# ScalarE casts ahead of their step's own work, modulation rows and residual chains at other steps, in a fused transformer layer

## The chip, the core and the metric

The kernel runs on one core of one Trainium2 chip. The metric is the device time of one execution in microseconds (us). A core has engines that run side by side, each through its own instructions in strict order: TensorE (PE in the profile, its weight loads PEld), VectorE (DVE), ScalarE (ACT), GpSimd (POOL) and SyncE (SP), which issues the DMA transfers. They wait for each other by semaphores.

## The reference, cut to what matters

One layer over 1024 latent tokens and 256 context tokens of width 1024, in float32: a half-weighted SwiGLU feed-forward block, attention of two kinds with gates and an output projection, and a second half-weighted SwiGLU block. Each sub-layer is normalised before and after, and shifted, scaled and gated by rows worked out from a conditioning vector ("modulation", nine rows of 1024 for each of the two streams).

```python
def _rmsnorm(x, g):
    y = x * lax.rsqrt(jnp.mean(x * x, axis=-1, keepdims=True) + RMS_EPS)
    return y * g
def _modnorm(x, g_pre, shift, scale):
    return _rmsnorm(x, g_pre) * (1 + scale) + shift
def _residual(x, y, g_post, gate, weight):
    return x + weight * gate * _rmsnorm(y, g_post)
def _swiglu(h, w1, w3, w2):                      # h @ w1, h @ w3: 1024 x 2816, w2: 2816 x 1024
    return (jax.nn.silu(h @ w1) * (h @ w3)) @ w2
```

The first block is applied to latents and to context, then one input projection of both, then the attention, the merge, and the second block on the latents.

## The kernel before, in words

**Products.** Each float32 operand is split into a high part (rounded to the format that TensorE multiplies at full rate, named fp32r in the profile) and a low part, the remainder. A product is three: high by high, high by low, low by high (`mm3`, L159). The split (`split_to`, L200) is two instructions: ScalarE casts the high part, VectorE then subtracts it from the source for the low part, so the second waits for the first. The latent products go by a Strassen-like scheme on 2 by 2 blocks with seven products for eight: a `Unit` (L497) stands for one weight tile pair, has the products `first`, `p6`, `second`, `p5`, `p7`, `p3`, `p4`, the differences t1 to t4 of its weight blocks (`sum`, on VectorE) and the splits of them and of blocks 11, 21 and 22.

**One order, written out by hand.** There is no scheduler: every instruction is pinned to its place in its engine's order. A `Plan` (L164) holds a list of main steps, mostly one product each, and for each step side work (`spread`), and `run` issues a step's main work and behind it the step's side work. Step numbers below are positions in the first plan:

| steps | stage | matmuls of a step |
|---|---|---|
| 0–36 | lead products of the first feed-forward block (ffn1) | 12 of 128x512 |
| 37–154 | ffn1's rest: 22 units, 5 steps each where led, else 7 (`plan_rest`, L636) | 12 of 128x512 |
| 155–231 | ffn1's down quarters: 7 quarters of 11 products over 4 banks (`Quarters`, L757) | 12 of 128x512 |
| 232–275 | context up: 22 column tiles by two matrices (`ctx_up`, L1082) | 24 of 128x256 |
| 276–319 | context down (`ctx_down`) | 6 of 128x512 |
| 320–424 | lead and rest of the input projection, 15 units | 12 of 128x512 |

The second plan later runs ffn2 in the same manner (22 units, then down quarters).

**Side work near the change.** In `plan_rest` a unit's `before` and `within` (L545 ff.) lay the splits and differences behind the steps of the unit before and of itself: both halves of a split stand behind the step's own work. That own work is, after the product, VectorE's sum out of a bank and, by `emit`, a Silu, Sigmoid or copy on ScalarE, which waits for that sum. `Quarters.plan` (L842 ff.) lays the split of operand n three steps ahead of product n, `Quarters.out` adds a finished quarter out of its bank on VectorE. In context up `ctx_split` splits a 128x1024 weight tile three steps ahead. `ada_steps` (L349) is the work on one modulation row: 23 entries, of which 16 load a 128x512 tile of the conditioning matrix and as many multiply-and-add it on VectorE (one instruction for each of the two streams; two entries behind its load), then `add_up` (small products into a bank and a copy out), then `turn`. Row 2 runs in ffn1's rest, row 4 at steps 185 to 231, row 3 at 234 to 268 with bank "v". The residual chains (`residual_steps`, L670; placed by `pos`) put a finished tile of 128 tokens through norm, gate and residual, and norm again: squares on ScalarE, two small instructions on POOL (mean and power), two 128x1024 instructions on VectorE, then the same for the second norm. Chains 0 to 3 stand at steps 210, 213, 216, 219, chains 4 to 7 at 229, 232, 235, 238. Banks carry the names bm, bv, bs, tiles the names of their pools: xv (16 wide), t (half tiles of 512), xu (units).

Of the kernel before, what the change touches and what calls it, by code (L numbers as in the profile page):

```python
# [9 lines left out]
F32R = mybir.dt.float32r  # L10
BF16 = mybir.dt.bfloat16
AF = mybir.ActivationFunctionType
ALU = mybir.AluOpType
# [17 lines left out]
NP = NF // 2  # L31
# [7 lines left out]
def f32(ap):  # L39
    return ap.bitcast(F32)  # L40
# [3 lines left out]
def hybrid_block(ctx: ExitStack, tc: tile.TileContext, a: dict, out: bass.AP):  # L44
# [11 lines left out]
    def nm(s):  # L56
        count[0] += 1
        return f"{s}_{count[0]}"
# [8 lines left out]
    def U(dt=F32, key="u"):  # L67
        return pools[key].tile([P, 1024], dt, tag="u", name=nm("x" + key))
# [7 lines left out]
    def T2(dt=F32, n=512):  # L76
        return pools["t"].tile([P, n], dt, tag="t", name=nm("t"))
# [34 lines left out]
    class Engine:  # L112


        def __init__(self, e):
            self.e = e
# [23 lines left out]
    def flush(before=None):  # L140
        while waiting and (before is None or waiting[0][0] <= before):
            put(*waiting.pop(0)[1:])
# [8 lines left out]
    vec, act, pool = Engine(nc.vector), Engine(nc.scalar), Engine(nc.gpsimd)  # L151
# [12 lines left out]
    class Plan:  # L164


        def __init__(self):
            self.main, self.side = [], {}

        def step(self, *fs):  # L170
            self.main += fs
# [2 lines left out]
        def spread(self, steps, first, last):  # L174

            for x, f in enumerate(steps):
                self.side.setdefault(first + x * (last - first) // len(steps), []).append(f)

        def run(self):
            for i, f in enumerate(self.main):  # L180
                clock[0] = i
                f()
                for g in self.side.pop(i, ()):
                    g()
                while deferred:
                    deferred.pop(0)()
                if owed:
                    owed.pop(0)()
                flush(i)
            assert not self.side  # L190
            clock[0] = None
            flush()

    def duo(n=512, key="u"):
        if key == "t":
            return T2(F32R)[:, :n], T2(F32R)[:, :n]
        t = U(F32R, key)
        return t[:, :n], t[:, 512:512 + n]

    def split_to(hi, lo, src):  # L200
        act.copy(hi, src)
        vec.tensor_tensor(lo, src, f32(hi), op=ALU.subtract)
        return hi, lo

    def split(src, n=512, key="u"):

        return split_to(*duo(n, key), src)

    def split2(src, key="u"):

        return split_to(U(F32R, key), U(F32R, key), src)
# [137 lines left out]
    def ada_steps(ms, tag="v"):  # L349

        s = []
        cur = {}

        def step(m, k, h):
            if m not in cur:
                cur[m] = AdaSum(m, tag)
            if k:
                cur[m].step(k - 1, h)
            if k < KD:
                cur[m].load(k, h)  # L360

        def end(m):
            cur[m].turn()
            if m == 4:
                cols["a1"] = scale_col("a1", 4, 2, 2)
            if m == 7:
                cols["a2"] = scale_col("a2", 7, 4, 1)

        for m in ms:
            s += [lambda m=m, k=k, h=h: step(m, k, h) for k in range(KD + 1) for h in range(2)]  # L370
            s += [lambda: None] * 2 + [lambda m=m: cur[m].add_up(), lambda: None, lambda m=m: end(m)]
        return s
# [124 lines left out]
    class Unit:  # L497
# [5 lines left out]

        def __init__(self, h, srcs, emit):
            self.h, self.srcs, self.emit = h, srcs, emit
            self.w, self.r = {}, {}
            self.led, self.fix = False, None

        def load(self, x, key="u"):
# [8 lines left out]
                self.m1 = T2()  # L518
                ld(self.m1, self.md)

        def split(self, name, key="u"):
            b = {"11": (0, 0), "21": (0, 1), "12": (1, 0), "22": (1, 1)}
            if name in b:
                x, o = b[name]
                src = self.r[x][:, o * 512:(o + 1) * 512]
            else:
                src = self.t[int(name[1]) - 1]
            self.w[name] = split(src, key=key)

        def sum(self, i):  # L530

# [12 lines left out]

        def before(self):  # L545

            first = {} if self.led else {"p7": lambda: self.split("11"), "p4": lambda: self.split("21")}
            return [("p5", lambda: self.sum(1)), ("p7", lambda: self.sum(2)), ("p7", lambda: self.split("t2")),
                    ("p3", lambda: self.split("t1")), ("p3", lambda: self.sum(3)), ("p4", lambda: self.split("t3"))] \
                + list(first.items())  # L550

        def within(self):

            return [("p6", lambda: self.sum(4)), ("p6", lambda: self.split("22")), ("p5", lambda: self.split("t4"))]

        def prod(self, bank, left, right, start, f=None, ks=range(4)):
            hi, lo = self.w[right]
# [78 lines left out]
    def plan_rest(plan, units):  # L636

        for i, u in enumerate(units):
            o = len(plan.main)
            e = plan.step(*u.rest())  # L640
            at = lambda n: o + u.names.index(n)
            for n, f in (u.within() if i else []) + (units[i + 1].before() if i + 1 < len(units) else []):
                plan.spread([f], at(n), at(n) + 1)
            if i + 2 < len(units):
                plan.spread([lambda v=units[i + 2], x=x: v.load(x) for x in (2, 0, 1)], e - 3, e)

# [110 lines left out]
    class Quarters:  # L757
# [12 lines left out]

        def __init__(self, w2, gated, ys):
            self.w2, self.gated, self.ys = w2, gated, ys
            self.b, self.ra, self.sp = {}, {}, {}
            self.n = 7 * NP

        def slot(self, name, p):
# [11 lines left out]
            t = self.ra[n] = T2()  # L788
            ld(t, self.gated.d[self.ORDER[n // NP][0], n % NP])

        def split(self, n, key="v"):
            a = split(self.ra.pop(n), key=key)
            self.sp[n] = a, split(self.slot(self.ORDER[n // NP][1], n % NP), key=key)

        def sum(self, name, p):
            out, x, y = {"t1": ("t1", "b12", "b11"), "t3": ("t3", "b22", "b12"),
# [45 lines left out]
        def plan(self, plan, ahead=3, loads=4):  # L842

            o = len(plan.main)
            at = lambda n: o + n
            for n in range(self.n):
                plan.spread([lambda n=n: self.load_a(n)], at(n) - ahead - loads, at(n) - ahead - loads + 1)
                x = min(at(n) - ahead, at(self.n - self.LAST) - 1)
                plan.spread([lambda n=n: self.split(n)], x, x + 1)
                plan.step(lambda n=n: self.step(n))  # L850
            for p in range(NP):
                for name, first in (("b11", 0), ("b21", NP), ("b12", 9), ("b22", 2 * NP + 2)):
                    x = at(first + p) - ahead - loads
                    plan.spread([lambda name=name, p=p: self.load_b(name, p)], x, x + 1)
                for name, x in (("t1", 4 + 4 * p // 3), ("t2", 2 * NP - 1 + 6 * p // 5), ("t3", 3 * NP + p), ("t4", 4 * NP - 1 + p)):
                    plan.spread([lambda name=name, p=p: self.sum(name, p)], at(x), at(x) + 1)
            return o
# [38 lines left out]
    first = [PB("s") for _ in range(3)]  # L896
# [22 lines left out]
    class Raw:  # L919

        us, f = {}, {}
# [57 lines left out]
    part = {}  # L979
# [37 lines left out]
    plan = Plan()  # L1017
# [24 lines left out]
    o = len(plan.main)  # L1042
# [22 lines left out]
    d1_at = down1.plan(plan)  # L1065
# [8 lines left out]
    cw, cr, cg, cc, cu = {}, {}, {}, {}, {}  # L1074

    def ctx_load(f, x):
        cr[f, x] = load(a[("f1w1", "f1w3")[x]][f], key="v")

    def ctx_split(f, x):
        cw[f, x] = split2(cr.pop((f, x)))  # L1080

    def ctx_up(f, x):  # L1082
        o = PB("m")[:, :NCTX]
# [45 lines left out]
        cols[f"g{v}"] = gate_rows(gcol[v], *x)  # L1129

    o = d1_at + 4 * NP
    plan.spread(ada_steps((4,)), d1_at + 30, d1_at + 7 * NP - 1)
    plan.spread([lambda v=v: gcol.update({v: gate_col(2, 1, v, 0.5)}) for v in range(2)], o + 2, o + 3)
    plan.spread([lambda: gate1(0, "u", "v")], o + 4, o + 5)
    e = len(plan.main)
# [4 lines left out]
    up_at = len(plan.main)  # L1140
    for f, x in ups:
        o = len(plan.main)
        plan.spread([lambda f=f, x=x: ctx_load(f, x)], o - 6, o - 5)
        plan.spread([lambda f=f, x=x: ctx_split(f, x)], o - 3, o - 2)
        plan.step(lambda f=f, x=x: ctx_up(f, x))
    down_at = len(plan.main)
    for e in range(2):
        for f in range(NF):
            o = len(plan.main)
            plan.spread([lambda f=f, e=e: ctx_wload(f, e)], o - 8, o - 7)  # L1150
            plan.spread([lambda f=f, e=e: ctx_wsplit(f, e)], o - 4, o - 3)
            plan.step(lambda f=f, e=e: ctx_down(f, e))
    plan.spread(ada_steps((3,)), up_at + 2, down_at - 8)
    plan.spread([lambda: gate1(1, "v")], down_at + 36, down_at + 37)
    pos = {}
    for j in range(4):
        pos[j] = d1_at + 5 * NP + 3 * j
        pos[4 + j] = up_at - 3 + 3 * j
    pos[8], pos[9] = len(plan.main) + 1, len(plan.main) + 2
    x1s = DR([NLAT, D])  # L1160
    xcs = DR([NCTX, D])
# [93 lines left out]
    for p in range(3):  # L1255
        punits.append(Unit(h2, [cq_src(2 * p), cq_src(2 * p + 1)],
                           lambda i, ci, x, bank, p=p: emit_cq(2 * p + i, ci, x, bank)))

    o = len(plan.main)
# [147 lines left out]
    o = len(plan.main)  # L1407
# [5 lines left out]
    for x, (c, s, ts) in enumerate(sets):  # L1413
        o = len(plan.main)
# [239 lines left out]
    o = va_at  # L1654
# [8 lines left out]
    o = len(plan.main)  # L1663
# [3 lines left out]
    o = len(plan.main)  # L1667
# [3 lines left out]
    o = len(plan.main)  # L1671
# [4 lines left out]
    o = len(plan.main)  # L1676
# [379 lines left out]
    plan = Plan()  # L2056
# [4 lines left out]
    for d in range(KD):  # L2061
        o = len(plan.main)
# [21 lines left out]
    plan = Plan()  # L2084
# [21 lines left out]
    at = {}  # L2106
# [8 lines left out]
    o = len(plan.main)  # L2115
# [13 lines left out]
    o = len(plan.main)  # L2129
# [62 lines left out]
    for j in range(4):  # L2192
        o = d2_at + 5 * NP + 2 * j
        plan.spread([lambda j=j: done2(j, 0)], o, o + 1)
        plan.spread([lambda j=j: done2(j, 1)], o + 1, o + 2)
        o = e - 9 + j
        plan.spread([lambda j=j: done_half(4 + j, 1)], o, o + 1)
        o = e - 4 + j
# [83 lines left out]
```

## Time and profile before

| what | value |
|---|---|
| median of the runs | 2597.57 us (2595.28 to 2597.59, 3 runs) |
| profiled execution | 2596.1 us |
| its span | 2594.3 us |
| mean granted TensorE clock | 0.998 |
| DMA over the span | 464.52 MB, mean 179 GB/s |

The profile is one execution on the chip. Its page gives each engine's busy time, and groups of instructions by line. Nearly every instruction of the other engines is recorded by one helper, L120, and nearly every matmul by L154, so groups are told apart by their tiles ("out<-in", with buffer numbers left out). Square brackets in a timeline give the idle time ahead of an instruction and what ended it. A line "A <- B" of the waits gives total us, times and longest us that engine and line A waited for B. Matmuls are pipelined and their ends are modelled, so a wait reads a little short where a matmul stands ahead of it.

### The profile page before, as it was taken

The page shows a single profiled execution, that of the slowest core. Times are in us where ns is not written, and L with a number is a line of the kernel's source. Part 1 is how long each engine was busy: PE and PEld are TensorE (multiplying, and loading weights), DVE is VectorE, ACT ScalarE, POOL GpSimd, SP SyncE. Part 2 cuts the span into 40 slices and gives each one's busy share as a digit, 9 for nine tenths or more (in the row PEclk, how much of TensorE's full clock was granted, in tenths as well). Part 3 has the DMA queues.
Part 4 walks back from the last instruction along what each step waited for, and adds up shares of the span by engine and source line. Part 5 has one row for each costly group of instructions (what it writes and reads, how often), then busy time and mean ns, then how long its engine had stood idle before and what let it go on. Part 6 is the DMA issues. An engine that isn't in the chain of part 4 may idle for free.

```text
span 2594.3 us, 38254 instructions
## 1 busy us (share of the span) xinstructions
PE 2548.6 (98%) x13464; PEld 2166.9 (84%) x13464; DVE 1885.7 (73%) x3552; ACT 1246.2 (48%) x2362; POOL 224.3 (9%) x368
## 2 busy tenths in 40 slices
PE   8999999999999999999999999999999999999998
PEld 6887778887899888789889999997788888888887
DVE  4788886679686577784469988886535788767777
ACT  6622223446544663333338977773246322323444
POOL 1000000002100000001003522221021000000003
PEclk9999999999999999999999999999999999999999
DMA  8445443935573576665987733206325444336814
GB/s 304 164 172 190 165 157 122 324 110 171 204 281 121 189 253 211 225 195 178 289 306 280 241 94 76 68 13 221 121 98 195 150 159 162 111 107 221 282 59 175
DMA packets 236976, 464.52 MB, mean 179 GB/s; under 512 B 29488, under 2 KB 70640, under 8 KB 236784
## 3 DMA queue, kind: packets, MB, share of 16 engines
q1 hardware_dynamic: 236784, 462.08, 52.6%
q8 instruction: 106, 1.74, 0.3%
q14 instruction: 86, 0.70, 0.1%
HBM read 341.33 MB, written 120.65 MB: 178 GB/s over the span
## 4 chain that ended last, share of the span: by engine, by line
PE 61%; issue 25%; DVE 7%; ACT 5%; DMA 1%; POOL 1%; SPq 0%; DVEq 0%; ACTq 0%; POOLq 0%
PE bs L154 25%; PE bm L154 20%; PE bv L154 12%; PE bm L157 2%; DVE t L120 2%; DVE xu L120 1%; ACT xu L1862 1%; DVE xv L120 1%; DVE xu L1726 1%; DVE t L1889 1%; ACT t L1888 1%; ACT xu L120 1%; PE bs L157 1%; POOL st L120 1%; ACT t L120 1%
## 5 line engine op out<-in xcount | busy, mean ns | idle before, releaser
L154 PE MATMUL bm<-xu,xu 128*128 128x512 f32 (+2 forms) x1584 | 368.8, 387 | 1.0 <-ACT t L120 0.9
L120 ACT CAST xu<-t 128x512 fp32r<-128x512 f32 (+1 forms) x282 | 167.1, 599 | 421.9 <-DVE t L120 405.3
L154 PE MATMUL bs<-xv,xu 128*128 128x512 f32 x1488 | 358.7, 390 | 8.3 <-DVE t L120 8.3
L154 PEld LDWEIGHTS bm<-xu,xu 128*128 128x128 f32 x1584 | 290.2, 188 | 59.1 <-ACT t L120 2.2
L154 PEld LDWEIGHTS bs<-xv,xu 128*128 128x128 f32 x1488 | 278.0, 188 | 71.5 <-issue 9.2
L154 PE MATMUL bv<-xv,xu 128*128 128x512 f32 x1342 | 335.7, 389 | 0.2
L154 PEld LDWEIGHTS bv<-xv,xu 128*128 128x128 f32 x1342 | 251.6, 188 | 53.2 <-issue 1.0
L120 DVE TENSOR_TENSOR xu<-t,xu 128x512 fp32r<-128x512 f32 (+1 forms) x282 | 187.9, 667 | 137.9 <-ACT xu L120 137.9
L154 PE MATMUL bs<-xv,xv 128*128 128x512 f32 x1014 | 250.6, 393 | 4.6 <-DVE xv L120 4.6
L154 PE MATMUL bs<-xu,xu 128*128 128x512 f32 (+1 forms) x1008 | 234.2, 382 | 0.6 <-DVE t L120 0.6
L120 DVE TENSOR_TENSOR xu<-xu,xu 128x512 fp32r<-128x512 f32 (+1 forms) x272 | 185.5, 688 | 60.3 <-ACT xu L120 59.9
L154 PEld LDWEIGHTS bs<-xv,xv 128*128 128x128 f32 x1014 | 190.6, 189 | 44.6 <-issue 5.4
L154 PEld LDWEIGHTS bs<-xu,xu 128*128 128x128 f32 x1008 | 184.1, 188 | 38.2 <-issue 2.2
L120 DVE TENSOR_TENSOR t<-t,t 128x512 f32<-128x512 f32 (+2 forms) x262 | 174.5, 673 | 50.1 <-ACT t L120 46.0
L154 PE MATMUL bs<-w,w 96*128 96x512 f32 (+3 forms) x832 | 206.3, 366 | 2.4 <-DVE st L1751 1.9
L120 POOL TENSOR_SCALAR st<-st 128x1 f32<-128x1 f32 (+1 forms) x66 | 38.6, 584 | 1922.0 <-ACT t L120 1906.9
L120 ACT ACTIVATE t<-t 128x512 f32<-128x512 f32 (+1 forms) x94 | 57.3, 610 | 232.0 <-DVE t L120 228.1
L120 ACT CAST xv<-t 128x512 fp32r<-128x512 f32 x154 | 95.7, 621 | 151.9 <-PE bv L154 65.5
L154 PE MATMUL bm<-t,xu 128*128 128x256 f32 (+1 forms) x1272 | 162.4, 289 | 4.3 <-DVE xu L120 2.7
L154 PE MATMUL bm<-xv,xv 128*128 128x512 f32 x618 | 165.1, 391 | 0.0
L154 PEld LDWEIGHTS bm<-t,xu 128*128 128x128 f32 x1272 | 158.2, 193 | 7.8 <-DVE xu L120 3.5
L154 PE MATMUL bv<-t,w 128*128 128x256 f32 x896 | 151.5, 288 | 2.5 <-DVE t L1889 1.8
(235 smaller groups left out, 4238.2 us busy)
## 6 DMA issues: line engine op xcount, KB each, us to landing
d<-t SPq DMA_DIRECT2D x338, 256.0 KB, 2.4
t<-d SPq DMA_DIRECT2D x246, 256.0 KB, 3.3
xu<-in_f1w SPq DMA_DIRECT2D x59, 512.0 KB, 3.9
xu<-in_f2w SPq DMA_DIRECT2D x58, 512.0 KB, 3.6
t<-in_wada SPq DMA_DIRECT2D x112, 256.0 KB, 3.9
xv<-in_f1w SPq DMA_DIRECT2D x44, 512.0 KB, 5.8
xu<-in_winT SPq DMA_DIRECT2D x38, 512.0 KB, 5.3
w<-d SPq DMA_DIRECT2D x32, 512.0 KB, 6.2
```

What stands on the lines that cost most here:

```text
L120: return lambda *x, **y: pin(f(*x, **y))
L154: return pin(nc.tensor.matmul(o, s, m, start=start, stop=stop, skip_group_check=open_group[0]))
L157: return pin(nc.tensor.transpose(o, x, i))
L1726: nc.vector.tensor_scalar(dst, src, 1.0, FMIN, op0=ALU.mult, op1=ALU.max, accum_out=m)
L1862: nc.scalar.activation(x, x, AF.Exp, bias=n_[:, s:s + 1], accum_out=l[:, i:i + 1])
L1888: nc.scalar.copy(t[0], pb)
L1889: nc.vector.tensor_tensor(t[1], pb, f32(t[0]), op=ALU.subtract)
```

## The change

It does three things. Every instruction stays; only places, buffers and waits move.

1. A plan has a second list, `early`, whose work is issued ahead of a step's main work. The casts of `plan_rest`'s splits, of `Quarters`' splits and of `ctx_split` go there, at the same step as before; the subtracts stay behind the step. In `before`, the difference t2 (`sum(2)`) goes from p7 to p5, the step ahead of it.
2. The modulation entries of row 4 go from steps 185–231 to 157–210, those of row 3 from 234–268 to 238–290 and from bank "v" to "m".
3. The residual chains 4 to 7 go from 229, 232, 235, 238 to 229, 235, 241, 247.

```diff
         def run(self):
             for i, f in enumerate(self.main):
                 clock[0] = i
+                for g in self.pre.pop(i, ()):
+                    g()
                 f()
                 for g in self.side.pop(i, ()):
                     g()
...
+    def low(hi, lo, src):
+        vec.tensor_tensor(lo, src, f32(hi), op=ALU.subtract)
+
     def split_to(hi, lo, src):
         act.copy(hi, src)
-        vec.tensor_tensor(lo, src, f32(hi), op=ALU.subtract)
+        low(hi, lo, src)
         return hi, lo
+
+    def cast(src, n=512, key="u"):
+        x = duo(n, key) if n <= 512 else (U(F32R, key), U(F32R, key))
+        act.copy(x[0], src)
+        return x, src
...
         def before(self):
-            first = {} if self.led else {"p7": lambda: self.split("11"), "p4": lambda: self.split("21")}
-            return [("p5", lambda: self.sum(1)), ("p7", lambda: self.sum(2)), ("p7", lambda: self.split("t2")),
-                    ("p3", lambda: self.split("t1")), ("p3", lambda: self.sum(3)), ("p4", lambda: self.split("t3"))] \
-                + list(first.items())
+            return [("p5", 1, None), ("p5", 2, None), ("p7", None, "t2"), ("p3", 3, "t1"), ("p4", None, "t3")] \
+                + ([] if self.led else [("p7", None, "11"), ("p4", None, "21")])
 
         def within(self):
-            return [("p6", lambda: self.sum(4)), ("p6", lambda: self.split("22")), ("p5", lambda: self.split("t4"))]
+            return [("p6", 4, "22"), ("p5", None, "t4")]
...
-            for n, f in (u.within() if i else []) + (units[i + 1].before() if i + 1 < len(units) else []):
-                plan.spread([f], at(n), at(n) + 1)
+            two = [(u, x) for x in (u.within() if i else [])]
+            if i + 1 < len(units):
+                two += [(units[i + 1], x) for x in units[i + 1].before()]
+            for v, (n, sum_, part) in two:
+                if part:
+                    plan.early(lambda v=v, part=part: v.cast(part), at(n))
+                    plan.spread([lambda v=v, part=part: v.low(part)], at(n), at(n) + 1)
+                if sum_:
+                    plan.spread([lambda v=v, sum_=sum_: v.sum(sum_)], at(n), at(n) + 1)
...
                 x = min(at(n) - ahead, at(self.n - self.LAST) - 1)
+                plan.early(lambda n=n: self.cast(n), x)
                 plan.spread([lambda n=n: self.split(n)], x, x + 1)
...
-    plan.spread(ada_steps((4,)), d1_at + 30, d1_at + 7 * NP - 1)
+    plan.spread(ada_steps((4,)), d1_at + 2, d1_at + 5 * NP)
...
+        plan.early(lambda f=f, x=x: ctx_cast(f, x), o - 3)
         plan.spread([lambda f=f, x=x: ctx_split(f, x)], o - 3, o - 2)
...
-    plan.spread(ada_steps((3,)), up_at + 2, down_at - 8)
+    plan.spread(ada_steps((3,), "m"), up_at + 6, down_at + 14)
...
         pos[j] = d1_at + 5 * NP + 3 * j
-        pos[4 + j] = up_at - 3 + 3 * j
+        pos[4 + j] = up_at - 3 + 6 * j
```

Here `d1_at` is 155, `up_at` 232, `down_at` 276 and `NP` 11.

More of the change, by code (lines that the diff above doesn't have):

```diff
@@ L167, in __init__ @@
         def __init__(self):
-            self.main, self.side = [], {}
+            self.main, self.side, self.pre = [], {}, {}
         def step(self, *fs):
@@ L177, in spread, with early @@
                 self.side.setdefault(first + x * (last - first) // len(steps), []).append(f)
+        def early(self, f, at):
+            self.pre.setdefault(at, []).append(f)
         def run(self):
@@ L189, in run @@
                 flush(i)
-            assert not self.side
+            assert not self.side and not self.pre
             clock[0] = None
@@ L505, in __init__ @@
             self.h, self.srcs, self.emit = h, srcs, emit
-            self.w, self.r = {}, {}
+            self.w, self.r, self.raw = {}, {}, {}
             self.led, self.fix = False, None
@@ L519, in load, with cast @@
                 ld(self.m1, self.md)
-        def split(self, name, key="u"):
+        def cast(self, name, key="u"):
             b = {"11": (0, 0), "21": (0, 1), "12": (1, 0), "22": (1, 1)}
@@ L527, in split, with low @@
                 src = self.t[int(name[1]) - 1]
-            self.w[name] = split(src, key=key)
+            self.w[name], self.raw[name] = cast(src, key=key)
+        def low(self, name):
+            low(*self.w[name], self.raw.pop(name))
+        def split(self, name, key="u"):
+            self.cast(name, key)
+            self.low(name)
         def sum(self, i):
@@ L772, in __init__ @@
             self.w2, self.gated, self.ys = w2, gated, ys
-            self.b, self.ra, self.sp = {}, {}, {}
+            self.b, self.ra, self.sp, self.raw = {}, {}, {}, {}
             self.n = 7 * NP
@@ L789, in load_a, with cast, split @@
             ld(t, self.gated.d[self.ORDER[n // NP][0], n % NP])
-        def split(self, n, key="v"):
-            a = split(self.ra.pop(n), key=key)
-            self.sp[n] = a, split(self.slot(self.ORDER[n // NP][1], n % NP), key=key)
+        def cast(self, n):
+            self.raw[n] = [cast(x, key="v") for x in (self.ra.pop(n), self.slot(self.ORDER[n // NP][1], n % NP))]
+        def split(self, n):
+            for x, src in self.raw[n]:
+                low(*x, src)
+            self.sp[n] = [x for x, src in self.raw.pop(n)]
         def sum(self, name, p):
@@ L1077, in ctx_load, with ctx_cast @@
         cr[f, x] = load(a[("f1w1", "f1w3")[x]][f], key="v")
+    def ctx_cast(f, x):
+        cr[f, x] = cast(cr[f, x], 1024)
     def ctx_split(f, x):
-        cw[f, x] = split2(cr.pop((f, x)))
+        cw[f, x], src = cr.pop((f, x))
+        low(*cw[f, x], src)
     def ctx_up(f, x):
```

## The prediction

> **What bounds the kernel now.** I read the page's first part, then the waits of TensorE, then the same waits and the counts of matmuls by stage, then the timeline around the longest waits.
>
> The page's first lines (busy us, share of the span, instructions):
>
> ```profile
> span 2594.3 us, 38254 instructions
> PE 2548.6 (98%) x13464; PEld 2166.9 (84%) x13464; DVE 1885.7 (73%) x3552; ACT 1246.2 (48%) x2362; POOL 224.3 (9%) x368
> L154 PE MATMUL bs<-xv,xu 128*128 128x512 f32 x1488 | 358.7, 390 | 8.3 <-DVE t L120 8.3
> ```
>
> TensorE bounds it, so only what makes TensorE wait or run at a lower clock can be won. The third line shows that a matmul is booked with 390 ns. Stages of the windows view (length, busy us with count for PE, PEld, DVE, ACT, POOL, then granted clock, DMA share, GB/s):
>
> ```profile
> 2030.00:2340.00 310.00, 310.00 (x1369) 256.68 (x1369) 231.19 (x365) 90.18 (x157) 0.00 (x0) 1.00 0.39 138
> 199.00:410.00 211.00, 203.90 (x896) 163.97 (x895) 176.61 (x283) 57.33 (x100) 0.00 (x0) 1.00 0.47 163
> 646.00:649.40 3.40, 0.40 (x2) 0.00 (x0) 2.92 (x4) 3.30 (x7) 3.06 (x5) 1.00 0.03 10
> 649.40:656.20 6.80, 5.37 (x13) 4.13 (x14) 6.80 (x11) 0.00 (x0) 1.83 (x3) 0.50 0.58 195
> 717.70:721.10 3.40, 1.23 (x9) 0.81 (x7) 2.41 (x4) 2.48 (x4) 0.00 (x0) 1.00 0.58 189
> 721.10:724.50 3.40, 3.22 (x15) 3.22 (x16) 2.93 (x6) 2.62 (x6) 0.92 (x2) 0.50 1.00 369
> 726.00:786.00 60.00, 60.00 (x501) 59.88 (x499) 50.03 (x68) 27.78 (x43) 0.00 (x0) 1.00 0.77 278
> ```
>
> At 2030-2340 a matmul starts every 310/1369 = 0.226 us: a wait ends 0.39-0.226 = 0.16 us later than its row says, since the matmul before it is booked too long. A step of 12 such matmuls takes 2.72 us; a context up step of 24 takes 24 x 60/501 = 2.87.
>
> The waits of TensorE in four stretches, in order 199-410 (ffn1's rest), 600-660 (its down quarters), 695-725 (context up, two lines), 959-1165 (the projection's rest):
>
> ```profile
> PE bs L154 <- DVE t L120: 6.8, 10, 1.3
> PE bs L154 <- DVE xv L120: 4.4, 1, 4.4
> PE bm L154 <- DVE xu L120: 2.7, 4, 0.8
> PE bm L154 <- ACT xu L120: 1.6, 1, 1.6
> PE bs L154 <- DVE t L120: 2.1, 4, 0.8
> ```
>
> With 0.16 for each: 6.8+1.6 = 8.4; 4.4+0.2 = 4.6; 2.7+1.6+0.8 = 5.1; 2.1+0.6 = 2.7. Sum 20.8 us. (Count as check: 896 x 0.226 = 202.9 of 211, so 8.1 lost.) Besides, after 649.4 and after 721.1 the clock was granted at 0.50: half of 5.37 and of 3.22 busy us is 2.7 and 1.6 us. All that this change can reach is 20.8+4.3 = 25.1 us, one per cent. A measurement here tells 0.2%, 5.2 us, from no change.
>
> **Edit 1: casts ahead of a step.** No operation is added or dropped; each cast changes its place in ScalarE's order and the subtract its distance from it. The timeline of a step in ffn1's rest:
>
> ```profile
> 257.49 0.63 ACT L120 ACTIVATE t<-t 128x512 f32<-128x512 f32 x1 [1.96 <-DVE t L120]
> 258.03 0.60 ACT L120 CAST xu<-t 128x512 fp32r<-128x512 f32 x1
> 258.66 0.69 DVE L120 TENSOR_TENSOR xu<-t,xu 128x512 fp32r<-128x512 f32 x1 [1.21 <-ACT xu L120]
> ...
> 261.76 0.69 DVE L120 TENSOR_TENSOR xu<-t,xu 128x512 fp32r<-128x512 f32 x1 [1.21 <-ACT xu L120]
> 262.37 1.41 DVE L120 SCALAR_TENSOR_TENSOR t<-t,sc,t 128x512 f32<-128x512 f32 x2
> 263.69 0.68 DVE L120 TENSOR_TENSOR t<-bs,t 128x512 f32<-128x512 f32 x1
> 264.53 0.47 PE L154 MATMUL bs<-xv,xu 128*128 128x512 f32 x1 [1.10 <-DVE t L120]
> ```
>
> The cast stands behind the sigmoid-linear unit's ACTIVATE, which waits for VectorE's sum; VectorE's subtract then waits 1.21 us for the cast, twice here. With the modulation pair of 1.41 behind it, p6's sum out of the bank starts only at 263.69, and p7, which writes the same bank, waits. Ahead of the ACTIVATE the cast needs only data that lie ready a step before. Groups of VectorE's work (busy, mean ns, idle ahead): the subtract at 199-410, the subtract and a sum out of a bank at 2050-2250:
>
> ```profile
> L120 DVE TENSOR_TENSOR xu<-t,xu 128x512 fp32r<-128x512 f32 x57 | 39.2, 688 | 28.8 <-ACT xu L120 28.8
> L120 DVE TENSOR_TENSOR xu<-t,xu 128x512 fp32r<-128x512 f32 x56 | 38.5, 688 | 27.6 <-ACT xu L120 27.6
> L120 DVE TENSOR_TENSOR t<-t,bs 128x512 f32<-128x512 f32 x28 | 19.1, 683 | 8.0 <-PE bs L154 8.0
> ```
>
> So 28.8 us of VectorE's idle time is freed against 8.4 us of TensorE's waits: late next would be the peak at p5 (a subtract and two sums, since t2's sum comes there from p7, at 0.61 us each by the start distance 261.76 to 262.37, its own sum, and 1.41 of modulation: 3.9 us in a step of 2.72), which the steps around it absorb. I count 8.1 of 8.4 (bounds 6 and 8.4) and by the same working 2.4 of 2.7 in the projection's rest (bounds 1.5 and 2.7). In ffn2's rest the same idle, 27.6, hides behind TensorE already (VectorE waits 8.0 for it): nothing.
>
> **Edit 2: modulation rows out of the down quarters' end.** Ahead of the wait of 4.4 us stand, in POOL's timeline, VectorE's, TensorE's, and the groups of VectorE at 618-648:
>
> ```profile
> 637.71 0.55 POOL L120 TENSOR_TENSOR st<-st,mhalf 128x1 f32<-128x1 f32 x1
> ...
> 642.84 3.35 POOL L120 TENSOR_TENSOR st<-st,mhalf 128x1 f32<-128x1 f32 x1
> ```
>
> ```profile
> 645.70 1.41 DVE L120 SCALAR_TENSOR_TENSOR t<-t,sc,t 128x512 f32<-128x512 f32 x2
> 647.54 1.28 DVE L120 SCALAR_TENSOR_TENSOR xv<-xv,st,xu 128x1024 f32<-128x1024 f32 x1 [0.44 <-POOL st L120]
> 648.86 1.23 DVE L120 TENSOR_TENSOR xv<-xv,xu 128x1024 f32<-128x1024 f32 x1
> 650.00 1.88 DVE L120 TENSOR_TENSOR xv<-xv,bs 128x512 f32<-128x512 f32 x3
> ```
>
> ```profile
> 650.83 1.62 PE L154 MATMUL bs<-xv,xv 128*128 128x512 f32 x3 [4.43 <-DVE xv L120]
> ```
>
> ```profile
> L120 DVE SCALAR_TENSOR_TENSOR t<-t,sc,t 128x512 f32<-128x512 f32 x12 | 8.4, 744 | 0.0
> ```
>
> That is 8.4 us of modulation on VectorE, which so late reaches the chain and, behind it, the sums out of the banks (650.00) that TensorE's last quarter overwrites. After the change the last of it stands at step 196 (entry 18 of 23 on steps 157 to 210), and the first chain at 210. If VectorE alone decided, more than 4.6 would come free; but the chain's first half follows POOL, whose power took 3.35 us here and 0.55 before, and the casts ahead of it on ScalarE. Bounds: nothing and 4.6. I take the two pairs next to it, 2.8, and the 0.4 of POOL's wait: 3.2, so 1.4 us stay. A wait of 1.4 leaves 2.0 busy us in a stretch of 3.4, while 1.23 was too little and 0.40 too: I take the clock as kept, 2.7 more (bounds nothing and 2.7).
>
> At its new place an entry comes every 53/23 = 2.3 steps, 0.6 us of VectorE for each 2.72: at 199-410 VectorE carries a denser load (176.6 of 211) beside the same work, so I take nothing. Its loads move with it in SyncE's queue, two entries ahead of use, 4.6 steps or 12.5 us. Landing rows at 790-830 and 685-700 (KB, us):
>
> ```profile
> t<-in_f1w SPq DMA_DIRECT2D x12, 256.0 KB, 2.9
> t<-in_wada SPq DMA_DIRECT2D x3, 256.0 KB, 8.0
> ```
>
> Even 8.0 is covered; if that cover went, one late load would cost what is over 12.5. Its last products, at step 203, now share a step and bank "v" with the first gate row, which must wait for the copy out of the bank. No row shows it; bounds 0 and 1.4 (a pair on VectorE ahead of the copy), I take 0.3.
>
> **Edit 3: context up.** The rows of one product pair:
>
> ```profile
> 710.29 1.05 ACT L120 CAST xu<-xv 128x1024 fp32r<-128x1024 f32 x1
> 710.41 0.42 DVE L120 TENSOR_TENSOR xu<-t,xu 128x256 fp32r<-128x256 f32 x1 [0.47 <-ACT xu L120]
> 711.37 1.23 DVE L120 TENSOR_TENSOR xu<-xv,xu 128x1024 fp32r<-128x1024 f32 x1 [0.53 <-ACT xu L120]
> ```
>
> VectorE per two steps (5.74 us): two subtracts of 1.23, the product's 0.41 (taken as the 0.42), 0.42: 3.3. Modulation, 1.41 per entry, 23 entries on 34 steps, 1.35 in two steps: 1.9; a chain's 1.28+1.23 per three steps: 1.7. Together 6.9, more than 5.74, with the subtract's 0.53 of idle behind the cast on top. After: 23 entries on 52 steps, 0.88 in two: 1.2; chains six steps apart, 0.8; together 5.3, and the cast no longer behind. The debt goes: I count 4.8 of 5.1 (bounds 3 and 5.1), and the half clock's 1.6 (bounds nothing and 1.6).
>
> The modulation's loads, 16 of 256 KB, now reach into context down, where fewer half tiles are free for the weights: the loads of steps 280 to 282, ahead in SyncE's queue, wait for the end of step 275. A down step has 6 matmuls, 1.36 us; four steps are 5.4. Landing 2.9, cast 0.6 and subtract 0.7 make 4.2: no wait. At the other row's 8.0 it would be 9.3, 3.9 late. Bounds 0 and 5; I take 0.3.
>
> **The sum.** 8.1 + 2.4 + 3.2 + 2.7 + 4.8 + 1.6 - 0.3 - 0.3 = 22.2 us. From the profiled execution's 2596.1 (span 2594.3 and 1.8 around it) that is 2573.9; the median of the runs is 2597.6, 1.5 higher, so I put the forecast between, 2574.5.
>
> By the Trainium skill, "TensorE: Matmul & The Clock Gate", "Part 1: The HAM clock gate", the clock falls only after at least one idle window of about 3.4 us. Here it fell behind 3.4 us with 1.23 us busy (717.7-721.1), so the measured row decides; by the page the term of 1.6 would not be there, and the forecast would be 2576.1.
>
> **Rivals.**
> A. POOL keeps the wait at the last quarter: the chain's first half follows POOL's power, VectorE's free time doesn't help, and 4.6 and the half clock stay. For it: 0.44 and the 3.35 us power; against: ScalarE and POOL themselves follow VectorE's chain before. 3.2+2.7 back: 2580.4. Chance 0.15. The Trainium skill, "SBUF — State Buffer", "Terms", says that VectorE and GpSimd lock a port pair for a whole instruction and the loser blocks; the power of 3.35 us, which ran beside VectorE's pair at 645.70, agrees as far as it goes, and no row shows the lock itself; a denser VectorE would lengthen such a power.
> B. Context down waits for its weights at step 280 as priced, 5 us: 2579.5. Chance 0.10.
> C. The change does not do what it says: VectorE's waits move to the next operation in its order, since sums still wait for TensorE (8.0 in the row above), and TensorE's waits stay: 2596. Against: 28.8 us of that idle is named for the cast alone. Chance 0.05.
> D. Slower. ScalarE's order is strict: a cast now at its head waits for VectorE's difference (t3's and t4's sum is only one step older). Once VectorE lags more than a step, 2.72 us, the ACTIVATE or copy that frees a bank waits behind it. Price: one cast, 0.6, per unit in 59 units (22, 15, 22), 35 us, with the gains of 10.5 in these stages lost too: 2574.5+35+10.5 = 2620. Against: at 199-410 VectorE is busy 176.6 of 211, and waits for TensorE at 2050-2250. Chance 0.07.
>
> **How the numbers follow.** Forecast 0.63, A 0.15, B 0.10, C 0.05, D 0.07. The forecast's own bounds: every term at its best, 25.1, gives 2571 and with the spread of the runs (2 us) 2569; with its lower bounds in edit 1 and 3 (4.8 less) 2579. A and B fall below 2581, both together 2586. I give 2568 to 2585, leaving out C, D and A with B. Faster by over 0.2% 0.88, within 0.05, slower 0.07.
>
> **What would show it.** In ffn1's rest the subtract's group shows near 0 idle behind the cast and the ten waits of 6.8 are gone; one wait of 0 to 2 us stays at the last quarter, with no slice at 0.50 behind it; no wait on xu in context up; ffn2's rest unchanged. It is wrong if the ACTIVATEs of ffn1's rest start later than VectorE's sums (D), if POOL is named ahead of the last chain (A), or if context down shows waits on a DMA (B).

## The result, and the profile after

The changed kernel takes 2572.4 us (median; 2571.4 to 2574.8), the kernel before 2596.7 beside it: ratio 0.9908, 95% interval 0.9891 to 0.9925. It is 24.3 us faster; the forecast was 2574.5.

The first lines of the page of the changed kernel:

```profile
span 2570.2 us, 38151 instructions
PE 2541.2 (99%) x13464; PEld 2165.0 (84%) x13464; DVE 1891.7 (74%) x3552; ACT 1252.9 (49%) x2362; POOL 218.3 (8%) x368
```

The five engines' counts are those of before, and so are VectorE's and ScalarE's busy times within 7 us: nothing was saved in work, the span lost 24.1 us of TensorE's waits and of its time at half clock. Of the lines of waits that the prediction lists (6.8, 4.4, 2.7, 1.6 and 2.1 us) one wait of 0.3 us is left in the changed kernel, in the projection's rest (the first line); the second line looks like that of step 221 but is a wait near the kernel's end, at 2532.7 us:

```profile
PE bs L154 <- DVE t L120: 0.3, 1, 0.3
PE bs L154 <- DVE xv L120: 0.3, 1, 0.3
```

The windows of the changed kernel: ffn1's rest, the end of the down quarters around step 221 (two rows), context up, context down. The same columns as before: length, busy time with count for PE, PEld, DVE, ACT, POOL, then granted clock, DMA share, GB/s:

```profile
199.00:410.00 211.00, 211.00 (x942) 173.59 (x941) 181.45 (x288) 60.34 (x103) 0.00 (x0) 1.00 0.49 166
626.00:642.00 16.00, 15.60 (x69) 12.45 (x67) 13.93 (x20) 12.21 (x22) 5.20 (x10) 1.00 0.80 290
642.00:656.20 14.20, 14.18 (x66) 11.57 (x67) 8.77 (x16) 11.95 (x23) 0.74 (x2) 1.00 0.10 38
671.30:798.00 126.70, 126.70 (x1058) 126.70 (x1057) 92.92 (x123) 67.15 (x104) 8.16 (x14) 1.00 0.65 239
798.00:863.70 65.70, 64.79 (x308) 52.31 (x307) 36.49 (x61) 32.91 (x58) 0.00 (x0) 1.00 0.65 221
```

and the last two stages of before:

```profile
686.80:822.00 135.20, 130.94 (x1075) 129.07 (x1074) 98.44 (x130) 66.52 (x105) 5.81 (x14) 0.99 0.63 228
822.00:885.60 63.60, 62.93 (x291) 51.94 (x289) 32.41 (x52) 31.86 (x56) 0.00 (x0) 1.00 0.66 218
```

At 199-410 TensorE starts 942 matmuls where it started 896, and the clock is 1.00 in every row. Context up is 8.5 us shorter. Context down is 2.1 us longer: 17 more matmuls lie in it and 17 fewer in context up, the products and transposes of modulation row 3, and a wait of its own is told below.

How the mechanism of ffn1's rest looks now, in the timelines of ScalarE and VectorE of the changed kernel, one step after the other (start, length, [idle ahead <- what ended it]):

```profile
252.94 0.63 ACT L120 ACTIVATE t<-t 128x512 f32<-128x512 f32 x1 [0.56 <-DVE t L120]
253.48 0.61 ACT L120 CAST xu<-t 128x512 fp32r<-128x512 f32 x1
254.68 0.63 ACT L120 ACTIVATE t<-t 128x512 f32<-128x512 f32 x1 [0.59 <-DVE t L120]
```

```profile
253.97 0.68 DVE L120 TENSOR_TENSOR t<-t,bv 128x512 f32<-128x512 f32 x1
254.57 0.68 DVE L120 TENSOR_TENSOR xu<-t,xu 128x512 fp32r<-128x512 f32 x1
...
257.58 1.41 DVE L120 SCALAR_TENSOR_TENSOR t<-t,sc,t 128x512 f32<-128x512 f32 x2
259.09 0.69 DVE L120 TENSOR_TENSOR t<-bs,t 128x512 f32<-128x512 f32 x1
```

ScalarE casts at 253.48, before the ACTIVATE at 254.68 that waits for VectorE's sum of 253.97; when VectorE comes to the subtract at 254.57, the cast has been done since 254.09 and there is no idle time. The modulation pair is still there (257.58), but the sum out of p6's bank follows at 259.09, as soon as TensorE has filled it (TensorE's p6 ended at 259.05). The groups of VectorE at 199-410:

```profile
L120 DVE TENSOR_TENSOR xu<-t,xu 128x512 fp32r<-128x512 f32 x58 | 39.7, 685 | 0.3 <-ACT xu L120 0.2
L120 DVE TENSOR_TENSOR t<-t,bs 128x512 f32<-128x512 f32 x29 | 19.8, 684 | 3.8 <-PE bs L154 2.9
L120 DVE TENSOR_TENSOR t<-bs,t 128x512 f32<-128x512 f32 x15 | 10.3, 689 | 11.6 <-PE bs L154 7.9 <-issue 3.6
```

28.8 us of idle time behind the cast are 0.3, and what VectorE waits for now is TensorE: in this stage the engine that bounds the kernel no longer waits, the other one does.

The same at step 221, in the changed kernel's timeline of VectorE: the sums out of the banks, which stood at 650.00 behind the chain in before, while TensorE stood idle from 646.4 on, now start at 636.96, ahead of the first matmul of step 221 at 638.39:

```profile
634.49 1.28 DVE L120 SCALAR_TENSOR_TENSOR xv<-xv,st,xu 128x1024 f32<-128x1024 f32 x1 [0.73 <-POOL st L120]
635.81 1.23 DVE L120 TENSOR_TENSOR xv<-xv,xu 128x1024 f32<-128x1024 f32 x1
636.96 1.88 DVE L120 TENSOR_TENSOR xv<-xv,bs 128x512 f32<-128x512 f32 x3
```

The stages, by the start of the first matmul of steps 37, 155, 200, 218, 232, 276, 320, 344 and 424 in each trace (us gained over before; the rest, at the start, where the first loads land, and in the later phases, comes to -0.8 to -3.5 in these profiles, and to -1.1 and -2.7 in the two repeats of before, so it is of the size of the scatter between executions):

| kernel | ffn1's rest | 200–217 | 218–231 | context up | context down | projection's rest |
|---|---|---|---|---|---|---|
| changed | +10.4 | -1.6 | +7.7 | +8.5 | -2.2 | +2.6 |
| e1, casts only | +10.4 | 0.0 | +0.2 | +4.6 | 0.0 | +2.6 |
| e2, moves only | 0.0 | -1.6 | +7.8 | +6.1 | -2.2 | 0.0 |
| e3, rest's casts only | +10.4 | 0.0 | +0.9 | +0.1 | 0.0 | +2.6 |
| e4, t2's difference only | +0.9 | 0.0 | +0.3 | +0.3 | 0.0 | -2.7 |
| e5, row 4 back | +10.4 | 0.0 | -0.7 | +8.5 | -2.2 | +2.5 |
| e6, chains back | +10.4 | -1.6 | +7.8 | +7.6 | -2.2 | +2.6 |
| e7, row 3 back | +10.4 | -1.6 | +7.8 | +5.9 | 0.0 | +2.6 |
| e10, three more moves | +10.4 | -1.5 | +8.7 | +8.5 | -1.8 | +2.6 |
| e13, before again | 0.0 | 0.0 | -0.8 | +0.1 | 0.0 | 0.0 |
| e14, before again | 0.0 | 0.0 | +0.5 | +0.3 | 0.0 | 0.0 |

Two pairs of entries belong together. Row 4's small products moved from stage 218–231 to step 203: between the starts of steps 222 and 232 the changed kernel gains 1.4, which is their place in before, and it loses 1.6 at 203. Row 3's moved from context up to context down, where it loses 1.5 between the starts of steps 280 and 290. In stage 218–231 the two repeats of before differ by 1.3, so smaller differences there tell nothing.

### The profile page after: what moved, and what is told of

Same layout as the page of the kernel before. It is cut to its first block, busy times and chain, and to the rows that moved or that the text cites. A ratio compares the mean times of both kernels' runs of the same rounds, so it can differ in the third digit from the quotient of the medians.

```text
span 2570.2 us, 38151 instructions
## 1 busy us (share of the span) xinstructions
PE 2541.2 (99%) x13464; PEld 2165.0 (84%) x13464; DVE 1891.7 (74%) x3552; ACT 1252.9 (49%) x2362; POOL 218.3 (8%) x368
## 4 chain that ended last, share of the span: by engine, by line
PE 64%; issue 24%; DVE 6%; ACT 5%; DMA 1%; POOL 0%; SPq 0%; DVEq 0%; ACTq 0%; POOLq 0%
PE bs L154 26%; PE bm L154 21%; PE bv L154 13%; PE bm L157 2%; ACT xu L1898 2%; DVE xu L1762 1%; DVE t L1925 1%; ACT t L1924 1%; DVE xu L120 1%; PE bs L157 1%; DVE t L120 1%; DVE xv L120 1%; ACT t L1898 0%; ACT t L1738 0%; ACT t L120 0%
## 5 line engine op out<-in xcount | busy, mean ns | idle before, releaser
L154 PEld LDWEIGHTS bv<-t,w 128*128 128x128 f32 x896 | 132.7, 189 | 18.4 <-DVE t L1925 6.8
```

Source lines behind the costliest of these rows:

```text
L154: return pin(nc.tensor.matmul(o, s, m, start=start, stop=stop, skip_group_check=open_group[0]))
```

## The experiments

The theory: three places, each with a cause of its own (casts in the rests; row 4 ahead of step 221; VectorE's load in context up). The main rival: one cause, VectorE's lost time behind the casts, for all of them.

**e1, the casts alone.** The changed kernel with

```diff
-    plan.spread(ada_steps((4,)), d1_at + 2, d1_at + 5 * NP)
+    plan.spread(ada_steps((4,)), d1_at + 30, d1_at + 7 * NP - 1)
-    plan.spread(ada_steps((3,), "m"), up_at + 6, down_at + 14)
+    plan.spread(ada_steps((3,)), up_at + 2, down_at - 8)
-        pos[4 + j] = up_at - 3 + 6 * j
+        pos[4 + j] = up_at - 3 + 3 * j
```

> Edit 1 alone: every early cast and the earlier t2 difference as changed; modulation rows 3 and 4 and chains 4 to 7 at their old steps. Theory (three places, three causes): ffn1's rest and the projection's rest gain as in the changed kernel, 10.4 and 2.6 us by the start times of their steps, the wait of TensorE at step 221 stays near 4.4 us with the half clock behind it, and context up keeps most of its 7 us of losses (I expect 2 of 7 back); about 2582. Rival (one cause): the casts free so much of VectorE that step 221 and context up clear as well; about 2574.

Measured: 2578.8 us (ratio 0.9931, 0.9914 to 0.9947), 18.0 less than before. Its waits of TensorE over the whole span, the line that holds step 221's (4.2) and that of context up:

```profile
PE bs L154 <- DVE xv L120: 4.9, 2, 4.2
...
PE bm L154 <- DVE xu L120: 1.5, 1, 1.5
```

The rests gain what the changed kernel gains, step 221 keeps its wait: the single cause falls. But the casts bring 4.6 in context up, where I gave them 2.

**e2, the moves alone.** The kernel before with the same three lines changed the other way.

> Edits 2 and 3 alone: rows 3 and 4 and chains 4 to 7 at their new steps, every cast and t2's difference as before. Theory: ffn1's rest and the projection's rest stay as before (ten waits of 6.8 us in 199-410), step 221 loses its wait of 4.4 us and the half clock behind it (6 us back), context up gains about 5 of 7; about 2586. Rival (one cause): with the casts late the waits stay at all three places; about 2596.

Measured: 2588.8 us (0.9970, 0.9959 to 0.9981), 8.0 less. The waits of TensorE that stay are those of the two rests (the first line), and in context up one line:

```profile
PE bs L154 <- DVE t L120: 8.7, 13, 1.3
...
PE bm L154 <- DVE xu L120: 1.5, 2, 1.3
```

No line with xv stands at 600-660: step 221 is clear without any early cast. In context up the moves bring 6.1, less the 1.5 of row 3's products 4.6. So casts (4.6) and moves (4.6) each bring two thirds of the 7.0 that both bring: they pay off the same debt, the work by which VectorE is behind TensorE there. The stages add up to 10.1 us where the medians give 8.0; the rest of this profile, -3.5, is the largest of all.

**e3, the casts of the rests alone.** e1 with the casts of the down quarters and of context up behind their step again:

```diff
-                plan.early(lambda n=n: self.cast(n), x)
-                plan.spread([lambda n=n: self.split(n)], x, x + 1)
+                plan.spread([lambda n=n: (self.cast(n), self.split(n))], x, x + 1)
...
-        plan.early(lambda f=f, x=x: ctx_cast(f, x), o - 3)
-        plan.spread([lambda f=f, x=x: ctx_split(f, x)], o - 3, o - 2)
+        plan.spread([lambda f=f, x=x: (ctx_cast(f, x), ctx_split(f, x))], o - 3, o - 2)
```

> Early casts and the earlier t2 difference in the rests of ffn1, the projection and ffn2 only; the casts of the down quarters and of context up behind their step, rows and chains at their old steps. Theory: 10.4 + 2.6 = 13 us back and nothing else; about 2584, with the wait of 4.4 at step 221. Rival (the quarters' casts matter): the same here, but the run with edit 1 alone is then faster by more than the 2 us that context up may bring.

Measured: 2584.9 us (0.9955, 0.9941 to 0.9970), 11.9 less, and the only stages that gain clear of the scatter are the two rests (10.4 and 2.6). Against e1 the quarters' casts bring nothing (stage 218–231: 0.9 here, 0.2 there) and context up's cast its 4.5. One more thing goes with the casts here: in p6 the changed kernel issues the subtract of block 22 ahead of t4's difference, where before issued it behind. No run takes that apart; the subtracts of such blocks (xu<-xu,xu) had no idle time ahead of them in before (0.0 at 199-410), so it can hardly be what brings the 10.4.

**e4, t2's difference alone.** The kernel before with

```diff
-            return [("p5", lambda: self.sum(1)), ("p7", lambda: self.sum(2)), ("p7", lambda: self.split("t2")),
+            return [("p5", lambda: self.sum(1)), ("p5", lambda: self.sum(2)), ("p7", lambda: self.split("t2")),
```

> Before, with one change: t2's difference at p5 in place of p7, every cast late. Theory: VectorE still waits for the casts, 28.8 us in 199-410, and only the order of its work shifts; within 2 us of before. Rival (the earlier difference is what takes the waits of ffn1's rest away): about 10 us faster, 2586.

Measured: 2598.3 us (1.0007, 0.9998 to 1.0017): no change. VectorE's subtracts at 199-410 and TensorE's waits in it:

```profile
L120 DVE TENSOR_TENSOR xu<-t,xu 128x512 fp32r<-128x512 f32 x58 | 39.9, 687 | 28.0 <-ACT xu L120 28.0
```

```profile
PE bs L154 <- DVE t L120: 6.3, 7, 1.7
```

The 28 us stay with the cast's place, and with them 6.3 of the 6.8 us of waits; the stage gains 0.9. By itself the earlier difference even costs 2.7 us in the projection's rest, where the waits rise from 2.1 to 4.0; why was not followed up.

**e5, row 4 back.** The changed kernel with the first two lines of e1's diff.

> The changed kernel with modulation row 4 back at steps 185 to 231. Theory (row 4 alone puts VectorE late at step 221): the wait of about 4.4 us at step 221 and the half clock behind it return, everything else as changed; about 7 us over the changed kernel, 2579. Rival (chains and row 3, whose work begins at 229 and 238, share the cause): the wait comes back by half or less, 2575.

Measured: 2577.8 us (0.9927, 0.9910 to 0.9943), 5.4 over the changed kernel. The wait of step 221 in its window, and the windows of the wait and of the time behind it:

```profile
PE bs L154 <- DVE xv L120: 5.0, 1, 5.0
```

```profile
635.20:640.20 5.00, 0.05 (x1) 0.01 (x1) 4.52 (x6) 3.48 (x7) 4.54 (x6) 0.88 0.02 5
640.20:647.00 6.80, 6.78 (x19) 5.35 (x20) 5.40 (x9) 0.92 (x3) 0.55 (x1) 0.58 0.61 195
```

Row 4 alone decides this wait, with the clock at 0.58 behind it. Net of the products' move its new place is worth 8.4 - 1.6 = 6.8 by the table, and 5.4 by the medians; the scatter of this stage is 1.3.

**e6 and e7, chains back, row 3 back.** The changed kernel with the third pair, or the second pair, of lines of e1's diff.

> The changed kernel with chains 5 to 7 back at three steps' distance. Theory (VectorE's load in context up: 3.3 of the products, 1.2 of row 3 and 1.7 of chains per two steps make 6.2 of 5.74 while chains run): waits of 1 to 3 us come back around steps 236 to 246; about 2574. Rival (with the cast ahead of its step the chains fit at any distance): no wait in context up, 2572.

> The changed kernel with modulation row 3 back at steps 234 to 268 and in bank v. Theory (3.3 + 1.9 + 0.8 = 6.0 per two steps of 5.74): 1 to 3 us of waits in context up, and the 0.85 of its products and the wait of 0.6 at step 279 leave context down; about 2573. Rival (row 3's distance matters as much as the chains' and takes most of the gain in context up with it): 5 to 7 us, 2578.

Measured: 2573.2 (0.9910, 0.9895 to 0.9925) and 2573.1 us (0.9911, 0.9897 to 0.9926), which the medians can't tell from the changed kernel. The waits of TensorE in context up, e6 and then e7, tell more:

```profile
PE bm L154 <- DVE xu L120: 0.7, 1, 0.7
```

```profile
PE bm L154 <- DVE xu L120: 0.7, 2, 0.6
```

So with the other parts in place the chains' distance brings 0.9 in context up, and row 3's 8.5 - 5.9 = 2.6 there, of which 2.2 come back in context down: 0.4. Both are at or under the low end that I expected; the casts are worth 8.5 - 6.1 = 2.4 in the same way.

**e10, three more moves.** The changed kernel with

```diff
+    def ctx_wcast(f, e):
+        cd[f, e] = cast(cd[f, e], key="t")
+
     def ctx_wsplit(f, e):
-        cv[f, e] = split(cd.pop((f, e)), key="t")
+        cv[f, e], src = cd.pop((f, e))
+        low(*cv[f, e], src)
...
+            plan.early(lambda f=f, e=e: ctx_wcast(f, e), o - 4)
             plan.spread([lambda f=f, e=e: ctx_wsplit(f, e)], o - 4, o - 3)
...
-    plan.spread([lambda: gate1(0, "u", "v")], o + 4, o + 5)
+    plan.spread([lambda: gate1(0, "u", "v")], o + 5, o + 6)
...
-    plan.spread([lambda k=k: steps[k]() for k in range(KD)], e - 11, e - 3)
+    plan.spread([lambda k=k: steps[k]() for k in range(KD)], e - 10, e - 2)
```

> The changed kernel with three more moves: context down's weight casts ahead of their step too, the context rows' fill one step later (so that step 221 has no transposes that wait for VectorE), the first gate row one step later than row 4's products. Theory (each wait left has the same cause, an operation behind late VectorE work in a strict order): the wait of 0.6 at step 279 and 0.9 at step 221 go and 0.3 at 203; about 1.5 us less, 2571. Rival (what is left there are the small products' own starts, not waits): unchanged, 2572.4.

Measured: 2570.4 us (0.9899 of before, 0.9884 to 0.9914). Its interval overlaps that of the changed kernel, so the runs alone don't separate the two; the stages give 1.0 at step 221, 0.4 in context down and 0.1 at 203, together 1.5 as expected. The reason for the wait at step 279 of the changed kernel was to be seen in its ScalarE and VectorE timelines:

```profile
801.14 0.41 ACT L120 CAST xu<-t 128x256 fp32r<-128x256 f32 x1 [2.42 <-DVE t L120]
801.45 1.66 ACT L120 CAST t<-t 128x512 fp32r<-128x512 f32 x3
```

```profile
799.36 1.41 DVE L120 SCALAR_TENSOR_TENSOR t<-t,sc,t 128x512 f32<-128x512 f32 x2
800.69 0.42 DVE L120 TENSOR_TENSOR t<-t,bm 128x256 f32<-128x256 f32 x1
```

It is the pattern of ffn1's rest once more: a pair of row 3, now so late, holds VectorE; ScalarE waits 2.42 us for the product of 800.69, and three weight casts stand behind. From start to start step 279 takes 2.01 us in the changed kernel and 1.66 in e10, where 1.36 is undisturbed (before): the cast ahead of its step takes half of the 0.65 away, not all of it.

**e11 and e12, VectorE made late on purpose.** The changed kernel with four, or six, sums at step 219 whose result nobody reads:

```diff
+    def idle_work():
+        t = T2()
+        for _ in range(4):
+            vec.tensor_tensor(t, ys[4][:, :512], ys[4][:, :512], op=ALU.add)
+    plan.spread([idle_work], d1_at + 64, d1_at + 65)
```

> The changed kernel with four sums of 128x512 that nobody reads put into VectorE's order at step 219: 2.4 us more ahead of the sums out of the banks at step 220. Theory (VectorE's lateness alone makes the wait at step 221, about 0.75 us of margin are left there): a wait of 1.5 to 2 us on VectorE at step 221. On the clock: by the rows of before, where 1.23 us busy of 3.4 were followed by half clock, the clock stays at 1.00, since some 1.5 us or more stay busy in any stretch of 3.4. Rival (waits of 1.8 us bring the half clock if they fall inside one such stretch): 0.50 in the stretch behind it.

> The same with six such sums, 3.6 us more: a wait of about 2.9 us at step 221. Theory: half clock behind it, some 2 to 3 us more lost than the wait itself. Rival (the clock falls only behind a whole stretch of 3.4 us without work): the clock stays at 1.00 and only the wait is lost.

Measured (one execution each): 2574.9 and 2576.8 us. From one matmul's start to the next, less the usual 0.23, the waits at step 221 are 1.35 and 2.80 us. The windows behind them, e11 (one) and e12 (wait and behind):

```profile
638.60:642.00 3.40, 2.97 (x12) 2.18 (x12) 3.40 (x6) 0.00 (x0) 0.00 (x0) 1.00 0.95 305
```

```profile
636.80:640.20 3.40, 0.81 (x4) 0.35 (x2) 3.37 (x5) 1.01 (x2) 0.67 (x1) 0.92 0.00 0
640.20:643.60 3.40, 3.34 (x9) 2.71 (x10) 3.40 (x6) 0.00 (x0) 0.00 (x0) 0.58 0.92 289
```

A wait of 1.35, a little under the 1.5 expected, leaves the clock at 1.00; one of 2.80 brings 0.58, so the rival that asked for a whole stretch of 3.4 us without work falls. The lateness alone makes the wait, and the margin of the changed kernel is 0.8 to 1.0 us (3.6 - 2.80 and 2.4 - 1.35). From start to start the matmuls at half clock lost 1.4 us, under the 2 to 3 expected, and net even that is not lost: stage 218–231 is 1.5 us longer in e12 than in e11, as much as the wait. In e11 two transposes at the end of step 221 wait 1.3 us for late VectorE; in e12, where TensorE comes later, they do not wait.

**e13 and e14, the kernel before twice more.**

> The kernel before, once more. Two kernels with the same waits of 1.8 and 0.9 us in context up differ in the clock behind them: 0.50 in one, full in the other. Theory (the clock is judged in stretches of its own, and it is chance how a wait lies in them): the half clock behind the wait of 4.4 us at step 221 comes again, that in context up comes in some executions and not in others. Rival (the length of a wait decides): both come again in each execution.

> The kernel before, a second time, with the same theories: half clock behind step 221 each time; in context up now and then by the theory, each time by the rival.

Measured: 2597.9 and 2598.1 us. The same wait in context up and the 3.4 us behind it, e13 and then e14:

```profile
718.90:722.30 3.40, 1.22 (x9) 0.81 (x7) 2.41 (x4) 2.47 (x4) 0.00 (x0) 1.00 0.58 188
722.30:725.70 3.40, 3.21 (x15) 3.21 (x16) 2.93 (x6) 2.62 (x6) 0.93 (x2) 0.55 1.00 323
```

```profile
717.70:721.10 3.40, 1.21 (x8) 0.80 (x7) 2.41 (x4) 2.49 (x4) 0.00 (x0) 1.00 0.57 183
721.10:724.50 3.40, 3.23 (x27) 3.23 (x28) 2.93 (x6) 2.63 (x6) 0.93 (x2) 1.00 1.00 375
```

The same kernel, the same busy 1.2 of 3.4 us, and once 0.55, once 1.00. Where the clock stayed, 12 more matmuls ran in those 3.4 us, and yet context up took as long within 0.2 us (+0.1 and +0.3 in the table). e3 and e4, which leave context up as in before, say the same: e4 had the half clock (0.52) and gains 0.3, e3 had full clock and gains 0.1. The waits of TensorE at 600-800 say why, e13 and then e14:

```profile
PE bm L154 <- DVE xu L120: 2.5, 4, 0.8
```

```profile
PE bm L154 <- DVE xu L120: 3.2, 7, 0.8
```

At full clock TensorE runs into three more waits for VectorE: VectorE was the bound there, and the half clock cost nothing that can be told from the scatter.

## Why the prediction was right

The mechanisms held, place by place; four terms were of another size or kind.

- **Edit 1, ffn1's rest: 8.1 forecast, 10.4 measured**, over the stated bound of 8.4. The term was mis-sized: the waits view booked ten waits, and stalls of under 0.3 us, which a modelled matmul end hides, don't stand in it. The check by counts (8.1 lost) agreed for a wrong reason: the window also holds short products of the modulation row, which fill the count. The two kernels' counts for the same window give it: 942 - 896 = 46 matmuls, by 0.226 us 10.4. e3 shows that the casts do it, e4 that t2's earlier difference alone does not.
- **The projection's rest: 2.4, measured 2.6. ffn2's rest: nothing, measured 0.00**, as VectorE's waits for TensorE said.
- **Edit 2: 3.2 + 2.7 - 0.3 = 5.6, measured 7.7 - 1.6 = 6.1.** The step that failed is the 1.4 us that were to stay: no wait of that kind is left. From start to start the wait of 4.6 ahead of step 221 is gone whole and so are 2.6 of half clock behind it, while 0.8 on two transposes at the step's end are new, and 0.2 more is lost at step 203 than the products took in their old place: 4.59 + 2.56 - 0.80 - 0.24 = 6.11. I left POOL's lateness in place, but POOL and ScalarE follow the chain's earlier half on VectorE and came forward with it: the power that releases the chain ended 4.0 us behind the start of step 220 in before (647.51 and 643.52) and ends 1.2 us ahead of it now (634.46 and 635.67). POOL is still named ahead of the chain (0.73), the sign that I gave for rival A, so that sign was no good: no wait of TensorE hangs on it. e5 shows that row 4 decides the wait: rival A falls. The clash of row 4's products with the gate row, put at 0.3, is at most those 0.24; the gate row one step later (e10) wins 0.1 of it.
- **Edit 3: 4.8 + 1.6, measured 8.5 less the 1.5 of products that only moved: 7.0.** The sum is near and its parts are not. The 1.6 for the half clock was no term: e13 and e14 show context up as long with it as without, within 0.2. The whole is VectorE's debt, 5.1 of it seen as waits and the rest, as e14 and e3 suggest, hidden behind the low clock. Of the three parts e6 and e7 leave the casts with the most (2.4), chains 0.9, row 3 0.4; with so much overlap none can be given a share of its own.
- **Context down: 0.3, measured 2.2 - 1.5 = 0.7.** Rival B's price was for weights that land late; what came are casts behind VectorE's row 3 pair (step 279); e10 takes half of it away.
- Rival C fell by the 0.3 us of idle behind the cast; rival D by e1: with every early cast no stage became slower. On the clock the Trainium skill's rule ("TensorE: Matmul & The Clock Gate", "Part 1: The HAM clock gate") asked for a whole idle window; e12's 2.80 us of wait were enough. That its window runs free, as the same section says, agrees with e13 and e14, though no run shows the window itself. By that rule the sum lacked the 1.6 and gave 2576.1; the term was worth nothing indeed, but because VectorE was the bound there, not for the Trainium skill's reason.

Together, from the profiled execution: 10.4 + 2.6 + 6.1 + 8.5 - 2.2 = 25.4, less 1.3 at the start and in the later phases, 24.1, where 22.2 was forecast.

## What to carry to other kernels

Where an engine's order is strict, a cheap first half of a two-engine pair (here a cast) belongs ahead of work that waits, and the gain is not the freed idle time of the second engine (28.8 us) but what the bounding engine waited for it (10.4). Read that from the matmuls' starts or from counts in the same window of two kernels, since short waits don't stand in the waits view. Where an engine off the bound is late by a debt, two edits that both pay it off don't add, and here a lower clock of the other engine during it cost nothing.

## What the runs showed of the hardware that was not expected

The half clock is not decided by the wait alone: with the same waits of 1.8 and 0.9 us in context up it came in the profile of before, in e13 and in e4 (1.23, 1.22 and 1.23 us busy of 3.4), and not in e14 and e3 (1.21 both). Behind the wait of over 4 us at step 221 it came in each of the seven profiles that have one, behind 2.80 (e12) it came in the one execution that there is, and behind 1.35 (e11) not. Why it differs between executions of the same work stays open.
